# A four-layer block on one core: modulation sums moved to TensorE, a norm read from PSUM, and two mixers in another order

## Chip, core and metric

The kernel runs on one core of one Trainium2 chip. The metric is the device time of one execution in microseconds (us). Engine names in the profile: PE is TensorE's matmuls, PEld its weight loads, DVE is VectorE, ACT is ScalarE, POOL is GpSimd, SP is SyncE, which issues most DMAs. SBUF is the memory that the engines work in, PSUM the one that TensorE writes to. "us" and "ns" are as printed.

## What is computed

A sequence of 512 tokens of width 1024 goes through four layers: one of differential attention beside a long convolution, one of multi-scale pooling, each with an MLP, and then two hybrid layers, each with a recurrent unit (RG-LRU) beside latent attention, and a gated feed-forward part. Everything is fp32. Of the reference, cut to what the change touches:

```python
def _modulate(h, shift, scale):
    return h * (1 + scale) + shift
...
    s_lat = jax.nn.silu(c)
    s_ctx = jax.nn.silu(c_ctx)
...
        mod_l = [m[:, None, :] for m in jnp.split(s_lat @ ada_w[i] + ada_b[i], N_MOD, axis=-1)]
        a_lat = _modulate(_rmsnorm(h_lat, norm1_g[i]), mod_l[0], mod_l[1])
...
            mod_c = jnp.split(s_ctx @ ada_w[i] + ada_b[i], N_MOD, axis=-1)
            a_ctx = _modulate(_rmsnorm(h_ctx, norm1_g[i]), mod_c[0], mod_c[1])
...
            p_lat = a_lat @ mix_w_in[e] + mix_b_in[e]
            q_l = _axial_rope(_split_q(p_lat), row, col)
            k_l, v_l = _split_kv(p_lat[..., KV_START:HY_START])
...
            k_c, v_c = _split_kv(kv_ctx)
            k_all = jnp.concatenate([k_c, k_l], axis=1)
            v_all = jnp.concatenate([v_c, v_l], axis=1)
            att_l = _diff_post(_diff_attn_blocked(q_l, k_all, v_all, lam), subln_g[e], lam_init)
...
def rg_lru(x, positions, w_a, b_a, w_x, b_x, a_param):
...
    mult = jnp.where(reset, 1.0, jnp.sqrt(-jnp.expm1(2.0 * log_a)))
    b_in = xf * i * mult
...
    _, h = lax.associative_scan(combine, (a, b_in), axis=1)
...
    y = jax.nn.sigmoid(gate_a) * y_a + jax.nn.sigmoid(gate_b) * y_b
```

## The kernel before

Activations lie transposed: a tile is 128 features by 512 tokens, eight tiles to the sequence. Each fp32 value is split into a high part and a rest, and a product is three matmuls, high by high, rest by high and high by rest (`mm3`, L458 to L460). Weights come from HBM in raw blocks of 512 KB through a ring of six buffers (`RAW_BUFS`), issued by SyncE in one order (`_dma_to`); ScalarE casts the high part (`_emit_h`, L255) and VectorE or GpSimd subtract the rest (`_emit_l`, L273). A buffer is issued anew when its block's part is done (`_done_part`). Big PSUM tiles are called `ps`; there are two small ones, `pss`. The order of the instructions on an engine is that in which the program is written; the table `PR` says at many places which of VectorE (V), GpSimd (G) and ScalarE (A) takes an operation, and how many steps of a side task run at a point.

**Modulation.** The sums `s_lat @ ada_w` come in halves of 512 columns. For each half four raw blocks of two slices come through the same ring; each slice of 128 by 512 is scaled by one column of `s_lat` and added to an accumulator (`_ada_step`, `scaled`, `add_scaled`: L371 on GpSimd, L373 on ScalarE, addition L383 on GpSimd). At the end VectorE transposes and reduces (`ada_sums`, L416 and L418), and TensorE puts the sums into columns (`flush`). Halves 4 to 9 of layer 0 run this way among the projections and the attention loop, one part whenever a weight is taken.

**The start.** `start` reads the tokens (x) and the context (ctx), takes statistics over eight tiles k, and sums the first shift, which needs the scaling of 32 slices, on GpSimd, VectorE and ScalarE by turns (L369, L371, L373, L378, L383). Then the reciprocal root (`rsqrt`) is broadcast by TensorE into PSUM and copied to SBUF (rb, rc), the shift's columns are summed (L1104, then `sh`, L1107), and the norm runs in passes: VectorE multiplies the eight tiles (L1120), ScalarE makes the high part (L1129), GpSimd and VectorE a second copy (L1130), and the rest is subtracted (L1124). After that come six outputs `out` and the eight context tiles (L1141 to L1144).

**Layer 0.** The query columns are computed in one gemm, then each of four keys with the sequence's tiles and, at once, with the context's. `v_shift` sums a shift for the values over eight tiles. Then an attention loop of 16 steps s follows: scores (L1500, L1505), the weights normalised and combined (`combine1`, L1527 and L1528), at every other step the transposes of the weights into two `pss` and one `ps` (L1541), their split (L1548, L1553), the product with the values, and one fill gemm of the long convolution's columns (`gemm1`).

**The hybrid mixers.** `conv2` and `conv` project and convolve, `lru_mm` makes the two gates of one block of the recurrent unit, `lru_exp` its decay (three operations of VectorE, L1977 to L1979), `lru_sqrt` the multiplier (ScalarE, L1986, with a table load), `lru_scan` the recurrence (VectorE, L1991). Two norms of the latents need a reciprocal root each (`rsqrt`, L548 to L556, ending in the tile ny; broadcast L563). Then eight heads run: a gate's gemm (`gate`, ScalarE's sigmoid L2101), the weights' transposes (`trans`), the next head's scores (softmax L2051 to L2056), a second gate, the product `pv`, and in even heads a query gemm split by L526 and L527. The four roots 0 to 3 stand ahead of the head loop, the scans 0 to 3 in head 0, roots 4 to 7 in head 1 and scans 4 to 7 in head 2.

## Time and profile before

| | us |
|---|---|
| median of 3 runs | 2636.95 (2635.93 to 2643.82) |
| profiled execution | 2637.4 |
| its span in the trace | 2635.6 |
| TensorE busy | 2467.1 (94%) |
| VectorE busy | 1826.1 (69%) |
| ScalarE busy | 1166.9 (44%) |
| GpSimd busy | 1413.7 (54%) |
| mean granted clock of TensorE, of full speed | 0.959 |

The start runs to about 130 us, projections of layer 0 to about 190, the attention loop to about 390, the rest of its mixer to about 450. The hybrid mixers lie at about 1230 to 1520 and 1940 to 2220 us. In a row of the timeline "x4" means four instructions of one line in a row, whose time is given from the first's start to the last's end; a bracket gives the time that the engine was idle before and what released it. A matmul's end is modelled, so that its pace is read from the starts.

### The profile page before, as it was taken

What the parts mean: (1) busy time and instruction counts of PE and PEld (TensorE: products, weight loads), DVE (VectorE), ACT (ScalarE), POOL (GpSimd) and SP (SyncE); (2) the same over time, 40 slices, a digit from 0 to 9 for tenths busy, and PEclk for the clock granted to TensorE, in tenths of its full rate; (3) what the DMA queues carried; (4) which work ended last, traced back from release to release, by engine and by line L of the source; (5) the groups of instructions that cost most, each with busy time, mean ns of one, the idle gap of its engine ahead of it and who ended that gap; (6) DMA issues with size and microseconds to landing.
All of it is one profiled execution on the core that took longest, in us unless ns stands there. A gap on an engine that the chain in (4) does not pass through costs nothing.

```text
span 2635.6 us, 32004 instructions
## 1 busy us (share of the span) xinstructions
PE 2467.1 (94%) x11496; PEld 2060.0 (78%) x11496; DVE 1826.1 (69%) x2649; ACT 1166.9 (44%) x2153; POOL 1413.7 (54%) x1120
## 2 busy tenths in 40 slices
PE   8787877999999999999879999999998899999998
PEld 6666666888888788888768888888887788888887
DVE  6899987786657797767788676455577876743334
ACT  3445653554434533335466544222346654523231
POOL 6687746277652489954564437878137735230001
PEclk8788988999999999999989999999989999999999
DMA  7233422376672366662212336666422123353321
GB/s 245 83 123 95 127 81 80 94 203 197 201 221 68 97 176 206 208 176 77 95 50 67 104 88 184 184 188 196 118 85 73 55 78 112 94 154 96 96 86 51
DMA packets 433367, 330.29 MB, mean 125 GB/s; under 512 B 11799, under 2 KB 365207, under 8 KB 433208
## 3 DMA queue, kind: packets, MB, share of 16 engines
q1 hardware_dynamic: 429976, 322.22, 41.2%
q0 software_dynamic: 3232, 6.03, 0.7%
q8 instruction: 90, 1.47, 0.2%
q14 instruction: 69, 0.57, 0.1%
HBM read 319.82 MB, written 8.39 MB: 125 GB/s over the span
## 4 chain that ended last, share of the span: by engine, by line
PE 71%; DVE 20%; ACT 3%; issue 3%; DMA 1%; POOL 1%; SPq 0%; DVEq 0%; ACTq 0%; POOLq 0%
PE ps L458 20%; PE ps L459 20%; PE ps L460 20%; PE ps L619 5%; PE ps L477 4%; DVE slot L273 1%; DVE slot L1991 1%; DVE slot L527 1%; DVE slot L1943 1%; PE ps L1385 1%; DVE slot L1553 1%; DVE slot L2056 1%; PE pss L574 1%; DVE slot L1979 1%; DVE mx L1501 1%
## 5 line engine op out<-in xcount | busy, mean ns | idle before, releaser
L458 PE MATMUL ps<-slot 128*128 128x512 f32 (+1 forms) x3024 | 1164.2, 385 | 55.3 <-DVE slot L527 16.8
L460 PE MATMUL ps<-slot 128*128 128x512 f32 (+1 forms) x3024 | 1156.1, 382 | 21.4 <-DVE slot L527 9.2
L459 PE MATMUL ps<-slot 128*128 128x512 f32 (+1 forms) x3024 | 1155.2, 382 | 3.9 <-POOL slot L273 1.7
L458 PEld LDWEIGHTS ps<-slot 128*128 128x128 f32 x3024 | 580.6, 192 | 168.7 <-DVE slot L527 19.6
L460 PEld LDWEIGHTS ps<-slot 128*128 128x128 f32 x3024 | 579.2, 192 | 131.5 <-DVE slot L527 9.5
L459 PEld LDWEIGHTS ps<-slot 128*128 128x128 f32 x3024 | 580.1, 192 | 109.0 <-POOL slot L273 2.6
L383 POOL TENSOR_TENSOR slot<-slot 128x512 f32<-128x512 f32 x336 | 490.0, 1458 | 128.2 <-ACT slot L373 102.5
L255 ACT CAST slot<-raw 128x512 fp32r<-128x512 f32 (+1 forms) x764 | 426.2, 614 | 271.3 <-DMA raw<-in_mlp_w_dram 147.9
L273 DVE TENSOR_TENSOR slot<-raw,slot 128x512 fp32r<-128x512 f32 x588 | 497.7, 891 | 24.4 <-ACT slot L255 23.1
L542 POOL TENSOR_TENSOR slot<-slot 128x512 f32<-128x512 f32 (+1 forms) x64 | 92.1, 1443 | 510.0 <-ACT slot L536 509.6
L273 POOL TENSOR_TENSOR slot<-raw,slot 128x512 fp32r<-128x512 f32 (+1 forms) x176 | 252.3, 1458 | 175.1 <-ACT slot L255 135.0
L371 POOL TENSOR_SCALAR slot<-raw,cols 128x512 f32<-128x512 f32 x192 | 199.5, 1042 | 117.1 <-DMA raw<-in_w_ada_dram 57.3
L536 ACT ACTIVATE slot<-slot 128x512 f32<-128x512 f32 (+1 forms) x98 | 55.4, 577 | 223.8 <-DVE slot L1716 69.4
L619 PE MATMUL ps<-slot 128*128 128x512 f32 x576 | 145.9, 413 | 6.0 <-DVE slot L1821 6.0
L371 POOL TENSOR_SCALAR slot<-raw,s_lat 128x512 f32<-128x512 f32 x96 | 113.8, 1189 | 62.2 <-DMA raw<-in_ada_w_dram 23.2
L2204 DVE TENSOR_TENSOR slot<-slot,ps 128x512 f32<-128x512 f32 x40 | 27.5, 688 | 172.1 <-PE ps L460 172.1
L619 PEld LDWEIGHTS ps<-slot 128*128 128x128 f32 x576 | 114.0, 200 | 31.5 <-DVE slot L1821 7.4
L526 ACT CAST slot<-slot 128x512 fp32r<-128x512 f32 x80 | 47.2, 622 | 182.5 <-DVE slot L2204 154.0
L477 PE MATMUL ps<-slot 128*128 128x512 f32 x480 | 111.1, 390 | 4.1 <-ACT slot L526 2.8
L477 PEld LDWEIGHTS ps<-slot 128*128 128x128 f32 x480 | 89.7, 188 | 23.8 <-ACT slot L526 3.2
L1716 DVE SCALAR_TENSOR_TENSOR slot<-ps,mod,slot 128x512 f32<-128x512 f32 x64 | 47.7, 746 | 82.0 <-PE ps L460 82.0
L527 DVE TENSOR_TENSOR slot<-slot 128x512 fp32r<-128x512 f32 x75 | 77.8, 1057 | 37.2 <-ACT slot L526 37.2
(321 smaller groups left out, 2768.0 us busy)
## 6 DMA issues: line engine op xcount, KB each, us to landing
raw<-in_mlp_w_dram SPq DMA_DIRECT2D x128, 512.0 KB, 5.3
raw<-in_w_ada_dram SPq DMA_DIRECT2D x96, 512.0 KB, 4.4
raw<-in_ada_w_dram SPq DMA_DIRECT2D x88, 512.0 KB, 4.6
raw<-in_w_ffn_in_dram SPq DMA_DIRECT2D x88, 512.0 KB, 4.4
raw<-in_w_in_dram SPq DMA_DIRECT2D x56, 512.0 KB, 3.8
raw<-in_w_ffn_out_dram SPq DMA_DIRECT2D x32, 512.0 KB, 5.1
raw<-in_mix_w_dram SPq DMA_DIRECT2D x20, 512.0 KB, 3.8
raw<-in_w_out_dram SPq DMA_DIRECT2D x16, 512.0 KB, 4.0
```

Source lines behind the costliest of these rows:

```text
L255: self.S.copy(r(v), src[:, k:k + kk, :])
L273: eng.tensor_tensor(r(lv), src, v, op=ALU.subtract)
L371: self.G.tensor_scalar(out, x, sc, 0.0, op0=ALU.mult, op1=ALU.add)
L383: self.G.tensor_tensor(out, out, v, op=ALU.add)
L458: self.PE.matmul(out, lhsT=wh, rhs=xh, start=start, stop=False)
L459: self.PE.matmul(out, lhsT=wl, rhs=xh, start=False, stop=False)
L460: self.PE.matmul(out, lhsT=wh, rhs=xl, start=False, stop=stop)
L477: self.PE.matmul(ps[:], lhsT=w[k][i], rhs=xs[k][j], start=(k == 0 and n == 0), stop=(k == kc - 1 and n == 2))
L527: (eng or self.V).tensor_tensor(r(l)[:, 0:n], src, h[:, 0:n], op=ALU.subtract)
L536: self.S.activation(sq[:, 0:n], x, AF.Square, scale=scale)
L542: (eng or self.G).tensor_tensor(st["acc"][:, 0:n], st["acc"][:, 0:n], sq[:, 0:n], op=ALU.add)
L619: PE.matmul(ps[:], lhsT=w[i][:, m * 128:(m + 1) * 128], rhs=r(x[j])[:], start=(k == 0 and n == 0), stop=(k == 7 and n == 2))
```

## The change

**Layer 0's modulation.** For halves 4 to 9 `_ada_rows` multiplies a raw slice on TensorE: the column of `s_lat` is broadcast to 32 stationary columns and the slice of 512 columns streams past; four slices go to the four 32-row parts of one `pss`. These are jobs: `gemm1` and the keys let one matmul of them in after every second k (`work(1)`) and what is left at the end. ScalarE copies the finished tile, and later `_ada_cols` adds the four parts up with 128 by 1 matmuls against `sel4`, two new columns of the constants. A raw block stays open until its job is done, which holds back the issue of the block that would take its buffer.

**The start.** The first shift is scaled by ScalarE and added by GpSimd; the value shift too. The norm goes tile by tile: VectorE multiplies by the broadcast in PSUM, ScalarE makes the high part, ScalarE or VectorE the copy in turns, VectorE the rest. The query columns and three keys run together over k, then the fourth key; the context's keys come last.

**The mixers.** One `rsqrt` over eight columns takes the place of two, its broadcast stands one gemm later; the roots, the exponentials and the scans are spread over the heads.

```diff
-    fs='GGVA',
-    vs='VA',
-    fstep=(1, 2, 1, 0, 0, 1, 0, 3),
+    fs='AAAA',
+    vs='AA',
+    fstep=(0, 1, 1, 0, 1, 2, 2, 1),
...
     def _done_part(self, p):
-        self._dma_to(p["idx"] + RAW_BUFS)
+
+        self.dma_want = max(self.dma_want, p["idx"] + RAW_BUFS)
+        self._dma_to(min([self.dma_want] + [i + RAW_BUFS - 1 for i in self.open]))
...
-        if kind == "ada":
+        if kind == "ada" and extra[0] == 0 and 4 <= extra[1] < 10:
+            self.open.append(p["idx"])
+            self.jobs.append(self._ada_rows(p, *extra[1:]))
+        elif kind == "ada":
...
+    def _ada_rows(self, p, half, i):
...
+        if i % 2 == 0:
+            self.bank = self.ps_s.tile([128, 512], F32, tag="pss", name="pss")
+        ps = self.bank
+        for k in range(2):
+            q = 2 * (i % 2) + k
+            self.PE.matmul(ps[32 * q:32 * q + 32, :], lhsT=self.s_lat[:, 2 * i + k:2 * i + k + 1].to_broadcast([128, 32]), rhs=p["raw"][:, k, :], start=True, stop=True)
+            yield
+        self.open.remove(p["idx"])
+        self._done_part(p)
+        if i % 2:
+            t = self.get()
+            self.S.copy(t[:], ps[:])
+            self.defer(lambda: self._ada_cols(t, half, i))
...
+    def _ada_cols(self, t, half, i):
+        ps = self.ps_s.tile([128, 512], F32, tag="pss", name="pss")
+        for j in range(4):
+            self.PE.matmul(ps[:, j:j + 1], lhsT=t[:, j * 128:(j + 1) * 128], rhs=self.sel4[:, 0:1], start=True, stop=True)
+        self.put(t)
+        m = self.mod[0][:, half * 4:half * 4 + 4]
+        self.V.tensor_tensor(m, ps[:, 0:4], self.col("ada_b", half * 4, 4) if i == 1 else m, op=ALU.add)
...
         for k, x in enumerate(xs):
             self.mm3(ps[:], w[k], x, k == 0, k == len(xs) - 1)
+            if k % 2:
+                self.work(1)
+        self.work()
...
-        bp, rb = self.bcast(y, 4, self.ps_s, "pss"), self.get()
-        S.copy(rb[:], bp[:])
-        bp, rc = self.bcast(y[:, 4:6], 2, self.ps_s, "pss"), self.get()
-        S.copy(rc[:, 0:TC], bp[:, 0:TC])
+        self.prefetch(3)
...
+        def norm(x, f, n, c_, hi, lo, k):
...
+            V.tensor_tensor(t[:, 0:n], x, f, op=ALU.mult)
+            S.activation(r(hi), t[:, 0:n], AF.Identity, scale=sc, bias=b)
+            if k % 2:
+                V.tensor_scalar(z[:, 0:n], t[:, 0:n], sc, b, op0=ALU.mult, op1=ALU.add)
+            else:
+                S.activation(z[:, 0:n], t[:, 0:n], AF.Identity, scale=sc, bias=b)
+            V.tensor_tensor(r(lo), z[:, 0:n], hi, op=ALU.subtract)
...
+        pss = keys(ws[0:3])
+        self.put(ws[0].tiles)
+        zq(0, pss[0])
+        for j in range(2):
+            ropes.append(self.rope(pss[1 + j], bin_(4 + j), rope))
+        ropes.append(self.rope(keys(ws[3:4])[0], bin_(6), rope))
...
-        yq = self.rsqrt(self.stat_ms(stq, 256, 1e-6), 4)
-        yk = self.rsqrt(self.stat_ms(stk, 128, 1e-6), 4)
         conv(2)
+        y = latent_rstd()
         lru_mm(0)
-        bq, bk = self.bcast(yq, 4), self.bcast(yk, 4)
         conv(3)
+        bq, bk = self.bcast(y, 4), self.bcast(y[:, 4:8], 4)
...
-        lru_sqrt(range(4))
...
             PT = trans(P)
+            if hd in (0, 3):
+                lru_sqrt(range(4) if hd == 0 else range(4, 8))
             P = scores(hd + 1) if hd < 7 else None
-            if hd < 2:
-                lru_exp(2 * hd + 4)
-                lru_exp(2 * hd + 5)
+            if hd in (1, 2):
+                lru_exp(2 * hd + 2)
+                lru_exp(2 * hd + 3)
             gb = gate()
-            if hd == 0:
-                lru_scan(range(4))
-            elif hd == 1:
-                lru_sqrt(range(4, 8))
-            elif hd == 2:
-                lru_scan(range(4, 8))
+            lru_scan(((0,), (1, 2), (3,), (4,), (5,), (6,), (7,), ())[hd])
```

How the rows of the engines move, at three places. Line numbers of the changed kernel are higher by 3 to 81 than those of before.

TensorE, the end of a fill gemm in the attention loop and the start of the product with the values behind it, before:

```order
L458 MATMUL ps<-slot 128x512
L459 MATMUL ps<-slot 128x512
L460 MATMUL ps<-slot 128x512
L458 MATMUL ps<-slot 128x256
L459 MATMUL ps<-slot 128x256
```

and now (L502 to L504 are `mm3`, L403 is `_ada_rows`):

```order
L403 MATMUL pss<-raw,s_lat 32x512
L502 MATMUL ps<-slot 128x512
L503 MATMUL ps<-slot 128x512
L504 MATMUL ps<-slot 128x512
L502 MATMUL ps<-slot 128x512
L503 MATMUL ps<-slot 128x512
L504 MATMUL ps<-slot 128x512
L403 MATMUL pss<-raw,s_lat 32x512 x5
L502 MATMUL ps<-slot 128x256
```

A raw slice now stands after every six matmuls of the gemm, and what is left of the jobs, five here, behind its last. Of the 48 such matmuls 12 come in the projections and 36 in the fill gemms of steps 1, 3, 5, 7, 9 and 13; 24 of the 48 stand in runs of four or five.

VectorE, the first head of a hybrid mixer between the softmax (its scaling L2056, now L2124) and the split of the query gemm (L527, now L574), before:

```order
L2056 TENSOR_SCALAR slot<-slot,sm_12200 128x512
L1977 TENSOR_TENSOR slot<-slot 128x512
L1978 SCALAR_TENSOR_TENSOR slot<-slot 128x512
L1979 SCALAR_TENSOR_TENSOR slot<-slot 128x512
L1977 TENSOR_TENSOR slot<-slot 128x512
L1978 SCALAR_TENSOR_TENSOR slot<-slot 128x512
L1979 SCALAR_TENSOR_TENSOR slot<-slot 128x512
L1991 SCALAR_TENSOR_TENSOR slot<-slot 128x512 x4
L527 TENSOR_TENSOR slot<-ps,slot 128x512 x2
```

and now:

```order
L2124 TENSOR_SCALAR slot<-slot,sm_12214 128x256
L2124 TENSOR_SCALAR slot<-slot,sm_12214 128x384
L2124 TENSOR_SCALAR slot<-slot,sm_12214 128x512
L2059 SCALAR_TENSOR_TENSOR slot<-slot 128x512
L574 TENSOR_TENSOR slot<-ps,slot 128x512 x2
```

Two exponentials' chains and three of four scans have left the place ahead of the split; the chains stand in heads 1 and 2 now.

ScalarE, around the roots (L1986, now L2054), the first gate (L2101, now L2182) and the casts of the weights' transposes (L2080, now L2148), before:

```order
L1961 ACTIVATE slot<-ps,cols 128x512 x4
L1986 ACT_TABLE_LOAD
L1986 ACTIVATE slot<-slot 128x512 x4
L255 CAST slot<-raw 128x512
L2101 ACT_TABLE_LOAD
L2101 ACTIVATE slot<-ps 128x512
L1961 ACTIVATE slot<-ps,cols 128x512 x2
L2080 CAST slot<-pss 128x512
```

and now:

```order
L2029 ACTIVATE slot<-ps,cols 128x512 x4
L258 CAST slot<-raw 128x512
L2182 ACTIVATE slot<-ps 128x512
L2029 ACTIVATE slot<-ps,cols 128x512 x2
L2148 CAST slot<-pss 128x512
L2148 CAST slot<-ps 128x384
L2148 CAST slot<-pss 128x256
L2148 CAST slot<-ps 128x128
L2054 ACT_TABLE_LOAD
L2054 ACTIVATE slot<-slot 128x512 x4
L2121 ACT_TABLE_LOAD
```

The four roots have moved behind the gate and the transposes, and the gate's table load ahead of the sigmoid is gone here.

## Rows read from the trace of the kernel before

**Rows 1.** The page's head: span, and each engine's busy time, share and instructions.
```profile
span 2635.6 us, 32004 instructions
PE 2467.1 (94%) x11496; PEld 2060.0 (78%) x11496; DVE 1826.1 (69%) x2649; ACT 1166.9 (44%) x2153; POOL 1413.7 (54%) x1120
```

**Rows 2.** Windows: stretch, us; busy (count) of PE, PEld, DVE, ACT, POOL; clock; DMA.
```profile
130.00:190.00 60.00, 49.32 (x224) 40.87 (x223) 59.14 (x74) 26.14 (x46) 52.03 (x36) 0.81 0.40 132
190.00:390.00 200.00, 160.74 (x773) 132.69 (x771) 180.81 (x297) 121.33 (x276) 126.92 (x101) 0.89 0.31 95
1230.00:1520.00 290.00, 260.20 (x1268) 218.65 (x1269) 220.33 (x366) 174.46 (x329) 153.50 (x126) 0.95 0.26 78
1940.00:2220.00 280.00, 255.93 (x1244) 215.23 (x1243) 213.26 (x332) 174.95 (x330) 153.12 (x127) 0.96 0.27 81
```

**Rows 3.** Waits of TensorE, 85 to 450 us: total, times, longest.
```profile
PE pss L1541 <- DVE slot L1528: 15.6, 4, 10.4
```

**Rows 4.** Timeline of VectorE: start, us, engine, line, operation.
```profile
127.28 2.49 DVE L527 TENSOR_TENSOR slot<-slot 128x512 fp32r<-128x512 f32 x4
157.43 5.83 DVE L527 TENSOR_TENSOR slot<-slot 128x512 fp32r<-128x512 f32 x4
```

**Rows 5.** Groups of GpSimd, 130 to 440 us: busy, mean ns, idle before.
```profile
L383 POOL TENSOR_TENSOR slot<-slot 128x512 f32<-128x512 f32 x49 | 72.0, 1471 | 35.3 <-ACT slot L373 31.8
L371 POOL TENSOR_SCALAR slot<-raw,s_lat 128x512 f32<-128x512 f32 x32 | 33.7, 1055 | 0.0
```

**Rows 6.** Timeline of the start: ScalarE, VectorE, TensorE.
```profile
72.28 5.01 ACT L373 ACTIVATE slot<-raw,s 128x512 f32<-128x512 f32 x8
...
87.31 7.33 DVE L378 SCALAR_TENSOR_TENSOR slot<-raw,s,slot 128x512 f32<-128x512 f32 x6
98.31 0.24 DVE L1107 TENSOR_TENSOR sh<-pss,cols 128x8 f32<-128x8 f32 x2 [3.66 <-PE pss L1104]
98.46 4.71 DVE L1120 TENSOR_TENSOR slot<-slot 128x512 f32<-128x512 f32 x7
...
113.42 1.22 DVE L1124 TENSOR_TENSOR slot<-slot 128x512 fp32r<-128x512 f32 x1 [0.68 <-POOL slot L1130]
...
126.94 0.43 DVE L1144 TENSOR_TENSOR slot<-slot 128x256 fp32r<-128x256 f32 x1
...
120.27 0.39 PE L460 MATMUL ps<-slot 128*128 128x512 f32 x1
```

**Rows 7.** Timeline of TensorE: fp32 matmuls in the input stage, start and value shift.
```profile
18.07 1.07 PE L920 MATMUL pss<-slot,hw 33*64 33x512 f32 x2
19.07 0.50 PE L458 MATMUL ps<-slot 128*128 128x512 f32 x1
...
88.65 1.95 PE L1104 MATMUL pss<-ones,slot 128*128 128x1 f32 x16 [0.46 <-ACT slot L1096]
...
190.45 1.88 PE L1169 MATMUL pss<-slot,ones 128*128 128x512 f32 x4
```

**Rows 8.** Waits of TensorE, first mixer; the last row: second mixer.
```profile
PE ps L458 <- DVE slot L527: 8.4, 4, 6.7
PE ps L458 <- ACT slot L2101: 7.4, 1, 7.4
PE ps L563 <- DVE ny L556: 6.4, 2, 5.4
...
PE ps L458 <- DVE slot L527: 8.4, 4, 6.6
```

**Rows 9.** Timeline of the first hybrid mixer's first head: ScalarE, VectorE, TensorE.
```profile
1340.87 0.63 ACT L1986 ACTIVATE slot<-slot 128x512 f32<-128x512 f32 x1 [2.37 <-DVE slot L1979]
...
1360.48 8.71 DVE L1991 TENSOR_TENSOR_SCAN slot<-slot 128x512 f32<-128x512 f32 x4
...
1369.83 0.58 PE L458 MATMUL ps<-slot 128*128 128x256 f32 x1 [6.67 <-DVE slot L527]
...
1374.79 0.39 PE L458 MATMUL ps<-slot 128*128 128x512 f32 x1
```

More of the change, by code (lines that the diff above doesn't have):

```diff
@@ L384, in add_scaled, with work @@
             self.put(t)
+    def _ada_rows(self, p, half, i):
[19 more added lines that the diff above has]
+        self.V.tensor_tensor(m, ps[:, 0:4], self.col("ada_b", half * 4, 4) if i == 1 else m, op=ALU.add)
+        if i == 3:
+            self.ready.add((0, half))
+    def work(self, n=None):
+        while self.jobs and n != 0:
+            if next(self.jobs[0], self) is self:
+                self.jobs.pop(0)
+            elif n:
+                n -= 1
     def _ada_step(self, p, layer, half, i):
@@ L520, in gemm1 @@
             self.mm3(ps[:], w[k], x, k == 0, k == len(xs) - 1)
+            if k % 2:
+                self.work(1)
+        self.work()
         self.put(w.tiles)
@@ L1131, in start @@
             A.append(hl)
             self.put(xs[k])
[L1133 to L1135 removed]
+            if k in (2, 4):
+                out(1 + k // 2)
+        bp = self.bcast(y[:, 4:6], 2, self.ps_s, "pss")
+        for i in range(4, 6):
             out(i)
[L1137 to L1138 removed]
+        self.prefetch(4)
         for k in range(8):
[L1140 to L1144 removed]
+            p = self.get()
+            norm(cx[k], bp[:, 0:TC], TC, 1, p[:, 0:TC], p[:, TC:2 * TC], k)
@@ L1145, in start @@
             AC.append(p)
-            self.put(t)
-        self.put(rc)
+        self.put(cxt)
         self.sh = sh
-        self.put(cxt)
-        next(self.filt)
         self.vw = vw
@@ L1220, in zq, with keys @@
             self.defer(lambda: Q.__setitem__(j, self.stack_put(a, True)), PR["zqd"])
-        zq(0, gemm1("q"))
+        look, self.look = self.look, 0
+        ws, ropes = [self.consume(n) for n in ("q", "k", "k", "k")], []
+        def keys(ws):
+            pss = [self.ps() for _ in ws]
+            for k in range(8):
+                for w, ps in zip(ws, pss):
+                    self.mm3(ps[:], w[k], axs[k], k == 0, k == 7)
+                if k % 2:
+                    self.work(1)
+            self.work()
+            return pss
+        pss = keys(ws[0:3])
[4 more added lines that the diff above has]
+        ropes.append(self.rope(keys(ws[3:4])[0], bin_(6), rope))
         self.l_eng = V
@@ L1232, in layer0 @@
             self.put(w.tiles)
-            a = self.rope(ps, bin_(4 + j), rope)
+            if j == 1:
+                self.prefetch(1)
+                for _ in range(8 - 2 * len(PR["tapk"])):
+                    next(self.filt)
+                next(self.filt)
+            a = ropes[j]
             t = self.get()
@@ L2096, in pv, with latent_rstd @@
             return po
+        def latent_rstd():
+            ps, ms = self.ps_s.tile([128, 512], F32, tag="pss", name="pss"), self.small(8, "ms8")
+            for i, st in enumerate((stq, stk)):
+                for t in range(4):
+                    PE.matmul(ps[:, 4 * i + t:4 * i + t + 1], lhsT=st["acc"][:, t * 128:(t + 1) * 128], rhs=self.ones[:, 0:1],
+                              start=True, stop=True)
+                self.put(st["acc"])
+            for i, width in enumerate((256, 128)):
+                cs = slice(4 * i, 4 * i + 4)
+                V.tensor_scalar(ms[:, cs], ps[:, cs], 1.0 / width, 1e-6, op0=ALU.mult, op1=ALU.add)
+            return self.rsqrt(ms, 8)
         def gate():
```

55 lines of the change are left out of this document (24 added, 31 removed).

## The prediction, made before the changed kernel ran

> **What bounds the kernel now.** I read the head of the page first, then the stage windows, then TensorE's waits, then single operations at the places of the edits. TensorE is busy 2467.1 of 2635.6 us [rows 1], so only some 168 us can be won without taking work from it. The windows show where these lie [rows 2]: of 130 to 190 us TensorE works 49.32, of 190 to 390 us 160.74, and there VectorE is the full engine (59.14 of 60, 180.81 of 200) with GpSimd busy for most of the time beside it (52.03 and 126.92). The two hybrid mixers leave it idle for 29.8 and 24.1 us. The longest kind of wait in layer 0 is that of the attention transposes for the weights that VectorE combines, 15.6 us in four pieces [rows 3]: VectorE sets the pace there.
>
> VectorE is slow because of GpSimd: the same four subtractions took 2.49 us at 127.28, when GpSimd was at rest, and 5.83 us at 157.43 beside it [rows 4]. That is 0.84 us more for one.
>
> **Modulation sums on TensorE.** The six halves are 24 raw blocks, 48 slices of 512 columns. Off GpSimd go 32 scalings of 1.055 us, 33.7 us, and of the 49 additions in the stretch some 35 (14 stay or come for the value shift) of 1.471 us, 51 us [rows 5]. From VectorE go twelve transposes and reductions (0.62 us each at the best, by the uncontended four of [rows 4]: 7.5 us) and eight steps of the value shift at 7.33 / 6 = 1.22 us [rows 6], 10 us. And each of 67 removed GpSimd operations may have held VectorE up by 0.84 us, at most 56 us; operations that read PSUM do not show the effect and part of GpSimd's time falls beside those, so I take half, 28 us, and keep 0 and 56 as ends. VectorE gets 17.5 + 28 = 46 us lighter, less twelve small additions, out of 240 us in 130 to 390 us.
>
> TensorE pays. No fp32 matmul with 32 output columns is in the trace; the nearest is L920 with 64 columns between two full matmuls. It starts at 18.07 and the next one at 19.07: 1.0 us. Two 128-column ones (L1169) took 1.88 us, 0.94 each [rows 7]. I take 1.0 because L920 has the narrow output and the neighbours of this case, 48 x 1.0 = 48 us. The 48 one-column matmuls that turn rows into columns are like L1104: 16 records, which are 8 matmuls of two passes each, in 1.95 us, so 0.24 us each and 12 us. Together 60 us, from 57 to 70.
>
> The Trainium skill speaks against this edit: its page TensorEngine Tiling (Array Packing), section Key Properties, says that a change of the tiling mode drains TensorE, and here single 32-column matmuls stand between 128-column ones. The trace shows what such a switch costs at L920: the matmul behind it took 0.50 us [rows 7] where its like takes 0.39 at full clock [rows 9], which would make 5 us more for 48 of them, within my upper end.
>
> Is there room? In 130 to 390 us TensorE is idle 260 - 210.06 = 50 us, and loses 0.19 of 49.32 and 0.11 of 160.74, 27 us, to a granted clock of 0.81 and 0.89 [rows 2], which comes back if it is kept busy. So 77 us of room for 60 us, if the waits on VectorE shrink by its 46 us. Then the loop is almost full on TensorE (143 + 48 = 191 of 200 at full clock), and no shorter than now. Two added waits work against it: a sum holds one of only two small PSUM buffers until ScalarE's copy, and the transposes of the weights, queued behind on TensorE, want both; and a raw block stays in the ring of six until its matmuls, so SyncE's next weight load waits. The DMA share of 0.31 to 0.40 in this stretch [rows 2] covers the second one. I put the loop at 0, from 12 us shorter to 15 us longer.
>
> **The start.** The first shift is now scaled by ScalarE alone (20 scalings behind the last input, of 5.01 / 8 = 0.63 us) and added by GpSimd alone, 18 additions of 1.471 us = 26.5 us. ScalarE begins at 72.28, so the sums come at about 100, where VectorE ended at 87.31 + 7.33 = 94.6 and the shift stood at 98.31 [rows 6]. With what ScalarE and GpSimd no longer do ahead of it this is a loss of some 2 us; the ends are 3 us won and 8 lost.
>
> The norm then reads the broadcast from PSUM and no GpSimd operation is left in it. Before, the eight tiles took from 98.46 to 113.42 + 1.22 = 114.6, and the context ones to 127.4 [rows 6]: 28.9 us. Now VectorE has 16 operations of 0.67 us (4.71 / 7 in the same rows), four of 0.7, then 16 of 0.43 and four of 0.4: 13.5 + 8.5 = 22 us, a gain of 7. The q columns and three keys run together over the tiles, so that by the end of the norm 96 full matmuls are done where 48 were done at 120.27; then VectorE's wait for context tiles no longer stops TensorE. That is worth at most 48 x 0.23 = 11 us, of which I take 6, since VectorE is the full engine behind it and 12 raw matmuls now stand there. Sum: 7 + 6 - 2 = 11 us won, from 0 to 20.
>
> **The hybrid mixers.** Their waits for other engines are listed in [rows 8]. The longest, 7.4 us in each mixer, is a gate's output that ScalarE could not take because four square roots stood ahead of it, and these waited for VectorE: the last began at 1340.87 after 2.37 us of it [rows 9]. Now the roots stand behind the weights' transposes of the first head, when their inputs are long done, and ScalarE has lost the two pairs of exponentials of that head: I take 6 of 7.4. The second, 6.7 us, is for a subtraction behind four scans (8.71 us from 1360.48) and two exponential chains of VectorE ahead of them. Now one scan is there and the chains are gone to the next two heads, where two scans at most stand in a row: 4.5 of 6.7. The third is the first mixer's reciprocal root: two chains in turn become one of the same length over eight columns, 4 of 6.4. After such a gap TensorE was at half clock, from 1369.83 to 1374.79 [rows 9], which loses half of 5 us; 3 us per mixer for its two gaps. That gives 4 + 6 + 4.5 + 3 = 17.5 and 6 + 4.5 + 3 = 13.5; less 1 us each for new small waits, 29 us. Ends: 16 us, if the moved chains and roots stop the next heads, and 36.
>
> **At nothing:** the wider constant and its small DMA (beside loads of weights), four squares' additions on VectorE in the input stage, and two table loads fewer per mixer on ScalarE, which isn't full. If uncovered, the squares cost 4 x 0.7 = 3 us.
>
> **Sum.** 11 + 0 + 29 = 40 us off the profiled 2637.4 us (2635.6 us and 1.8 around it): 2597 us. The median of the runs is 2636.95, half a microsecond off, which I leave.
>
> **Rivals.** (1) The hybrid gaps only move: VectorE has the same work in 290 us and has 220.33 of it now [rows 2]; chains and scans of the later heads come to stand before subtractions that TensorE wants. Then 8 of 29 remain: 2618 us. Against it: the waits are of bursts, not of a full engine. Chance 0.12. (2) GpSimd's leaving doesn't speed VectorE, as its ScalarE-fed additions for the value shift stay beside it: VectorE then gets only 17 us lighter, the loop is held by both, 12 us longer, 2609 us. Against it: the two rows of [rows 4]. Chance 0.09. (3) Runs of four and five raw matmuls at the ends of gemms overlap, each in its own 32 columns: 24 of the 48 would take the time of 6, 18 us less on TensorE, of which the loop gives back 12: 2585 us. Nothing in the trace has such neighbours. Chance 0.10. The same page and section of the Trainium skill says that different tiles can run matmuls in parallel; no row here shows it. (4) The slower side: TensorE becomes the bound of layer 0. The raw matmuls stand inside the gemms whose results the next scores wait for, in order, and the two small PSUM buffers force the transposes to wait for sums. If none of the 60 us falls into the idle 50, all are added: 2597 + 60 = 2657 us. It decides from 40 us on the path; 48 make it slower by 0.3%. For it: DMA, copy and buffer tie the engines closely. Against it: VectorE gets lighter in the same stretch. Chance 0.07. The forecast has 0.62.
>
> **Range and chances.** The bounds of the three terms give 2637 - 20 - 12 - 36 = 2569 and 2637 + 15 - 16 = 2636; not all fall together, and I take 2572 to 2624, which holds rivals 1, 2 and 3 as well and leaves out the slower one and corners of the forecast, some 0.2. A measurement of this kernel can tell 0.3% from no change, 7.9 us. The forecast puts 0.60 of its 0.62 on faster, rival 1 0.11, 2 0.07, 3 0.10: 0.88 faster, 0.06 the same, 0.06 slower.
>
> **What would show it.** Right: TensorE over 0.93 busy at a clock near 0.95 from 190 to 390 us with the loop's end within 15 us of before, a 32-column matmul of about 1.0 us start to start, GpSimd's busy time in 130 to 390 us down by some 80, the four subtractions nearer 2.5 us, the context tiles' norm ended by about 121, and no wait over 3 us in the hybrid mixers. Wrong: the transposes waiting for sums' buffers by tens of microseconds; shift sums past 108; new waits of 5 us in heads 1 to 3.

## The result, and the profile after

The changed kernel takes 2661.7 us (median of 4 runs, 2657.3 to 2664.6) against 2637.4 us of before in the same comparison: ratio 1.0087, 95% interval 1.0072 to 1.0101. It is 24 us slower. The forecast was 2597 us and faster, and the time lies above the whole range.

The head of the page after (busy us, share of the span, instructions), to be read against [rows 1]:

```profile
span 2662.6 us, 32281 instructions
PE 2502.4 (94%) x11680; PEld 2065.7 (78%) x11680; DVE 1790.1 (67%) x2630; ACT 1183.0 (44%) x2183; POOL 1286.0 (48%) x1018
```

The stage windows after (stretch, us; busy us and count of PE, PEld, DVE, ACT, POOL; clock; DMA share; GB/s), to be read against [rows 2]:

```profile
130.00:190.00 60.00, 38.78 (x177) 27.45 (x175) 49.47 (x67) 34.60 (x62) 27.07 (x17) 0.80 0.17 55
190.00:390.00 200.00, 174.66 (x826) 126.78 (x826) 129.42 (x273) 106.51 (x242) 49.53 (x41) 0.92 0.30 92
1230.00:1520.00 290.00, 268.34 (x1300) 225.53 (x1299) 237.05 (x362) 170.71 (x317) 162.57 (x128) 0.96 0.25 73
1940.00:2220.00 280.00, 263.46 (x1275) 221.43 (x1274) 223.76 (x346) 168.50 (x319) 150.28 (x121) 0.96 0.26 77
```

The relief came as forecast: VectorE, busy before for 180.81 of the 200 us from 190 to 390, is busy for 129.42 of them, and GpSimd for 49.53. But TensorE lost 10.5 us of work in 130 to 190 us, and has 14 us more in the loop, with the added matmuls. What it waits for in layer 0 (85 to 450 us: total, times, longest):

```profile
PE ps L502 <- ACT slot L573: 19.3, 1, 19.3
PE pss L403 <- issue: 14.9, 5, 7.8
PE pss L1150 <- POOL slot L392: 12.8, 1, 12.8
PE ps L504 <- DVE slot L574: 7.9, 1, 7.9
```

The 15.6 us of the transposes [rows 3] are gone. The first two lines are new: a gemm that waits for a cast on ScalarE (L573), and the raw matmuls themselves (L403).

When each stage starts, against before, for the same matmul in both traces: the first scores begin at 206.58 instead of 177.58 (+29.0), layer 0 ends 41 us later, the first hybrid mixer gives back about 5 and the second about 9, and the end is 27.0 us later (spans 2662.6 and 2635.6). Nearly all of the miss is in layer 0. I call "shift of layer 0" how much later the same gemm matmul, counted from the first, starts behind layer 0, some 455 us into before; it comes from one profiled execution of each kernel.

### The profile page after: what moved, and what is told of

The parts are those of the page before. It is cut to its first block, busy times and chain, and to the rows that moved or that the text cites. A ratio compares the mean times of both kernels' runs of the same rounds, so it can differ in the third digit from the quotient of the medians.

```text
span 2662.6 us, 32281 instructions
## 1 busy us (share of the span) xinstructions
PE 2502.4 (94%) x11680; PEld 2065.7 (78%) x11680; DVE 1790.1 (67%) x2630; ACT 1183.0 (44%) x2183; POOL 1286.0 (48%) x1018
## 4 chain that ended last, share of the span: by engine, by line
PE 75%; DVE 14%; ACT 5%; issue 3%; DMA 1%; POOL 1%; SPq 0%; DVEq 0%; ACTq 0%; POOLq 0%
PE ps L502 21%; PE ps L503 21%; PE ps L504 21%; PE ps L666 4%; PE ps L521 3%; PE pss L403 1%; DVE slot L2011 1%; DVE slot L279 1%; DVE slot L2047 1%; PE pss L621 1%; PE ps L1453 1%; DVE slot L574 1%; ACT slot L258 1%; ACT slot L716 1%; PE ps L2115 1%
## 5 line engine op out<-in xcount | busy, mean ns | idle before, releaser
L502 PE MATMUL ps<-slot 128*128 128x512 f32 (+1 forms) x3024 | 1167.7, 386 | 48.3 <-ACT slot L573 19.3
L504 PE MATMUL ps<-slot 128*128 128x512 f32 (+1 forms) x3024 | 1153.9, 382 | 8.6 <-DVE slot L574 7.9
L502 PEld LDWEIGHTS ps<-slot 128*128 128x128 f32 x3024 | 580.0, 192 | 186.9 <-issue 24.1
L504 PEld LDWEIGHTS ps<-slot 128*128 128x128 f32 x3024 | 578.9, 191 | 116.8 <-DVE slot L574 8.1
L392 POOL TENSOR_TENSOR slot<-slot 128x512 f32<-128x512 f32 x308 | 452.5, 1474 | 163.3 <-ACT slot L382 142.8
L589 POOL TENSOR_TENSOR slot<-slot 128x512 f32<-128x512 f32 (+1 forms) x60 | 82.8, 1384 | 507.4 <-ACT slot L583 507.0
L573 ACT CAST slot<-slot 128x512 fp32r<-128x512 f32 x80 | 47.3, 619 | 191.6 <-DVE slot L2280 153.9
L380 POOL TENSOR_SCALAR slot<-raw,s_lat 128x512 f32<-128x512 f32 x64 | 77.8, 1220 | 61.5 <-DMA raw<-in_ada_w_dram 23.2
L574 DVE TENSOR_TENSOR slot<-slot 128x512 fp32r<-128x512 f32 x75 | 79.4, 1079 | 36.6 <-ACT slot L573 36.6
```

The lines of the kernel that those rows point to most:

```text
L380: self.G.tensor_scalar(out, x, sc, 0.0, op0=ALU.mult, op1=ALU.add)
L392: self.G.tensor_tensor(out, out, v, op=ALU.add)
L502: self.PE.matmul(out, lhsT=wh, rhs=xh, start=start, stop=False)
L504: self.PE.matmul(out, lhsT=wh, rhs=xl, start=False, stop=stop)
L574: (eng or self.V).tensor_tensor(r(l)[:, 0:n], src, h[:, 0:n], op=ALU.subtract)
L589: (eng or self.G).tensor_tensor(st["acc"][:, 0:n], st["acc"][:, 0:n], sq[:, 0:n], op=ALU.add)
```

## Experiments

**The three edits alone.** Each of these is the kernel before with one edit. In the first, `_ada_rows`, `_ada_cols` and `work` of the change, with the keys of the old projection order:

```diff
             self.mm3(ps[:], w[k], x, k == 0, k == len(xs) - 1)
+            if k % 2:
+                self.work(1)
+        self.work()
```

> The kernel before with the modulation sums on TensorE alone: start, order of the projections, engine table and mixers as before, the raw matmuls let into gemms and keys after every second k. Theory A (TensorE's order and the two small PSUM buffers cost more than VectorE's relief brings): 12 to 18 us longer, 2650 to 2655 us, with waits of the raw matmuls of about 15 us in the attention loop. Theory B (the loss in layer 0 is that of the start, which moves the whole loop; the sums by themselves give what GpSimd and VectorE lose): 10 us shorter or more, 2627 us.

Measured: 2658.2 us, ratio 1.0068 [1.0051, 1.0086], +17 us; layer 0 shifts by +22. VectorE falls to 125.35 us busy in 190 to 390 us and TensorE rises to 175.43. The relief is there, and the kernel is slower all the same, with TensorE the busy engine. That is my fourth rival, in part.

The second has the start: the first shift on ScalarE and GpSimd, the norm tile by tile, the projections' order, and with it the filter's steps behind the keys. Three entries of the table `PR` go with it: the query weights' subtractions (`l_q`) move from GpSimd to VectorE and the side task's steps are spread otherwise (`side`), neither of which I had priced, and the squares of the statistics (`sx`, `sc`) all go to VectorE, which I had put at nothing. None of them was run alone.

```diff
-    fs='GGVA',
+    fs='AAAA',
...
+            V.tensor_tensor(t[:, 0:n], x, f, op=ALU.mult)
+            S.activation(r(hi), t[:, 0:n], AF.Identity, scale=sc, bias=b)
...
+            V.tensor_tensor(r(lo), z[:, 0:n], hi, op=ALU.subtract)
```

> The kernel before with the changed start alone: first shift on ScalarE and GpSimd, norm tile by tile from PSUM, keys together, context keys last, filter steps behind them, engine table; sums on GpSimd and ScalarE and mixers as before. In the trace of the changed kernel the norm ends 13.5 us later and one wait of 19.3 us for the filter's split stands behind it. Theory A (the parts add): the first scores come 25 us later or more, and the whole is 20 to 30 us longer, 2660 us. Theory B (VectorE and GpSimd catch up in the attention loop, which was bound by them): 5 to 10 us longer, 2645 us. The forecast had 11 us shorter.

Measured: 2661.9 us, 1.0074 [1.0055, 1.0092], +21 us; layer 0 +26. My 11 us won were 26 lost. TensorE's waits of this run, 85 to 450 us:

```profile
PE ps L494 <- ACT slot L562: 22.1, 1, 22.1
PE pss L1596 <- DVE slot L1583: 13.0, 6, 8.0
PE pss L1137 <- POOL slot L384: 12.8, 1, 12.8
```

L494 and L562 are the lines of `mm3` and of the cast here: the long wait belongs to the start's edit, with no raw matmul on TensorE. The third has the mixers' edit:

```diff
-            if hd < 2:
-                lru_exp(2 * hd + 4)
-                lru_exp(2 * hd + 5)
+            if hd in (1, 2):
+                lru_exp(2 * hd + 2)
+                lru_exp(2 * hd + 3)
...
+            lru_scan(((0,), (1, 2), (3,), (4,), (5,), (6,), (7,), ())[hd])
```

> The kernel before with the change of the two hybrid mixers alone (one reciprocal root, roots, exponentials and scans spread). My forecast was 29 us shorter. The trace of the changed kernel has the matmuls of the first mixer come 5 us nearer to those of before over that mixer and those of the second 8.6 us nearer. Theory A (the three parts add): 13 to 14 us shorter, 2624 us. Theory B (the mixers are disturbed by what layer 0 leaves behind, the ring of raw blocks above all): 25 us or more shorter, 2612 us.

Measured: 2617.2 us, 0.9912 [0.9895, 0.9929], 24 us faster, near the forecast of 29. In its trace the mixers give 7 and 12 us.

**What a raw matmul costs.** Two stretches of TensorE in the kernel after (start, us, engine, line, operation and tile):

```profile
177.90 0.28 PE L504 MATMUL ps<-slot 128*128 128x256 f32 x1
178.11 1.06 PE L403 MATMUL pss<-raw,s_lat 128*32 128x512 f32 x8
179.10 0.50 PE L502 MATMUL ps<-slot 128*128 128x512 f32 x1
...
180.36 0.40 PE L504 MATMUL ps<-slot 128*128 128x512 f32 x1
180.69 1.04 PE L403 MATMUL pss<-raw,s_lat 128*32 128x512 f32 x2
181.67 0.50 PE L502 MATMUL ps<-slot 128*128 128x512 f32 x1
182.00 0.40 PE L503 MATMUL ps<-slot 128*128 128x512 f32 x1
```

Two records are one fp32 matmul. Four in a row take 1.06 us, one alone takes 1.04: the four run side by side, each in its own 32 columns. The one alone also costs around it: from 180.36 to 182.00 are 1.64 us for it and two 128-column matmuls, which without it start 0.23 us apart, so about 1.2 us are its own. The Trainium skill's page TensorEngine Tiling (Array Packing), section Key Properties, says that different tiles can execute matmuls in parallel, and that a change of the tiling mode drains TensorE. This trace agrees: four cost one, and around a single one some 0.2 us are lost beside its own 0.98 from start to start; that this loss is the drain, no run shows. So the next run leaves the arithmetic as it is and lets the raw matmuls stand only behind a whole gemm:

```diff
             self.mm3(ps[:], w[k], x, k == 0, k == len(xs) - 1)
-            if k % 2:
-                self.work(1)
         self.work()
```

> As the one with the sums on TensorE alone, but no raw matmul stands inside a gemm: all that are ready run behind it, four or eight in a row. In the trace of the changed kernel four in a row took 1.08 us from start to the next matmul's start (178.02 to 179.10), as much as one by itself, so that TensorE would pay 12 times 1.1 us instead of 24 times 1.2 us and 5 runs, some 25 us less. Theory A (the price on TensorE and in its order decides): 15 to 25 us shorter than with single ones. Theory B (the small PSUM buffers decide, which are asked for as often): within 5 us of it.

Measured: 2625.0 us, 0.9941 [0.9920, 0.9961], 16 us faster than before and 33 us faster than the singles; layer 0 -11. Its raw matmuls now stand in runs such as:

```profile
161.60 0.39 PE L504 MATMUL ps<-slot 128*128 128x512 f32 x1
161.92 1.92 PE L403 MATMUL pss<-raw,s_lat 128*32 128x512 f32 x16
163.77 0.38 PE L502 MATMUL ps<-slot 128*128 128x256 f32 x1
```

Eight in 1.85 us. Is it the overlap, or that the sums' small PSUM buffers are asked for at better times? The same kernel with 128 equal columns for each raw matmul keeps the place and takes the overlap away (the four parts of a bank then overwrite each other):

```diff
-            self.PE.matmul(ps[32 * q:32 * q + 32, :], lhsT=self.s_lat[:, 2 * i + k:2 * i + k + 1].to_broadcast([128, 32]), rhs=p["raw"][:, k, :], start=True, stop=True)
+            self.PE.matmul(ps[:], lhsT=self.s_lat[:, 2 * i + k:2 * i + k + 1].to_broadcast([128, 128]), rhs=p["raw"][:, k, :], start=True, stop=True)
```

> As the kernel with the sums in runs behind the gemms, but each raw matmul has 128 stationary columns instead of 32, over the whole small buffer, so that none can run beside another; each overwrites the one before, so the halves' sums are not those of the reference. Theory A (the gain of the runs is TensorE's time: four at a time against one after the other): 48 times 0.86 us = 41 us on TensorE in place of some 13, so 20 to 28 us longer than with 32 columns, 2648 us, as much as with single ones. Theory B (the gain is that of the small buffers, which are held for a shorter time): within 6 us of the narrow one, 2628 us.

Measured: 2646.1 us, 1.0028 [1.0016, 1.0040], +7.5 us. By the ratios 23 of the 33 us are lost again, with the raw matmuls where they were; by the shifts of layer 0 (+6 against -11) it is 17. Its rows:

```profile
163.04 0.39 PE L504 MATMUL ps<-slot 128*128 128x512 f32 x1
163.26 7.03 PE L403 MATMUL pss<-raw,s_lat 128*128 128x512 f32 x16
169.73 0.68 PE L502 MATMUL ps<-slot 128*128 128x256 f32 x1
```

Eight take 6.47 us instead of 1.85. The three kernels make a ledger. Column two adds up every stretch of L403 from its first start to the next matmul's start; three is the L403 wait of the list of waits; the 48 column matmuls (L415) are 11 us in each, 0.23 each by the 1.84 us that eight took in the kernel after:

| kernel | 48 raw matmuls, us | their waits | all added | shift of layer 0 | won on the path |
|---|---|---|---|---|---|
| sums_only | 37.1 | 14.2 | 62 | +22 | 40 |
| sums_wide_grouped | 39.7 | 2.8 | 53 | +6 | 47 |
| sums_grouped | 11.4 | 3.5 | 26 | -11 | 37 |

The last column is what GpSimd's and VectorE's relief was worth: 37 and 40 us with 32 columns, and 47 in the wide kernel. There TensorE was granted 0.94 and 0.95 of its clock in 130 to 190 and 190 to 390 us, in sums_grouped 0.91 and 0.92; by my estimate from these that is 8 of the 10 us between the two. So the relief differs less than the price, 62, 53 or 26 us, and the price sets the sign. Of the 33 us between singles and runs, 17 to 23 are lost with the overlap; the rest goes with the waits, 14.2 us against 3.5 and 2.8, and with the switches, which the wide matmuls, of as many columns as their neighbours, don't have either. The longest of the waits, in the kernel after, is this one:

```profile
246.90 1.03 PE L403 MATMUL pss<-raw,s_lat 128*32 128x512 f32 x1 [7.83 <-issue]
```

and VectorE, at the same time:

```profile
245.73 0.47 DVE L1596 SCALAR_TENSOR_TENSOR slot<-slot,rc 128x256 f32<-128x256 f32 x1
246.12 1.27 DVE L1621 TENSOR_TENSOR slot<-pss,slot 128x512 fp32r<-128x512 f32 x2
```

The first raw matmul of a sum opens a small buffer. Both were held by transposes whose subtraction (L1621) stood behind the softmax on VectorE; when the first of the two was done, at about 246.8, TensorE went on. The profile names no releaser ("issue"); that it is the buffer is read from this coincidence and from the tile's name, pss. I had foreseen the transposes waiting for the sums. It was the other way round, inside a gemm, with everything of TensorE queued behind.

**The start.** VectorE in the norm after (the bracket is the idle time before, and what ended it):

```profile
104.04 0.24 DVE L1153 TENSOR_TENSOR sh<-pss,cols 128x8 f32<-128x8 f32 x2 [0.24 <-PE pss L1150]
105.06 0.69 DVE L1165 TENSOR_TENSOR slot<-slot,pss 128x512 f32<-128x512 f32 x1 [0.79 <-PE pss L610]
107.40 0.69 DVE L1171 TENSOR_TENSOR slot<-slot 128x512 fp32r<-128x512 f32 x1 [1.65 <-ACT slot L1170]
108.01 0.68 DVE L1165 TENSOR_TENSOR slot<-slot,pss 128x512 f32<-128x512 f32 x1
108.72 0.55 DVE L1168 TENSOR_SCALAR slot<-slot,gg,sh 128x512 f32<-128x512 f32 x1
109.68 0.69 DVE L1171 TENSOR_TENSOR slot<-slot 128x512 fp32r<-128x512 f32 x1 [0.41 <-ACT slot L1166]
...
125.33 0.69 DVE L1171 TENSOR_TENSOR slot<-slot 128x512 fp32r<-128x512 f32 x1 [0.36 <-ACT slot L1166]
```

A tile's subtraction (L1171) follows its multiplication (L1165) on the same engine and needs ScalarE's two results of it, so VectorE stands still for 1.65 us on every second tile and about 0.4 on the others. From 104.04 to the end of the last subtraction are 22.0 us, 21.0 of them from the first multiplication on, and the context tiles take to 140.85. The waits ahead of L1171 add up to 8.1 us in the eight tiles and 5.7 in the context's. Two theories of the 29 us: this chain, or the filter's cast behind it. In the first kernel each subtraction is issued behind the next tile's multiplication:

```diff
-            V.tensor_tensor(r(lo), z[:, 0:n], hi, op=ALU.subtract)
-            self.put(t, z)
+            self.put(t)
+            if late:
+                late.pop()()
+            def rest():
+                V.tensor_tensor(r(lo), z[:, 0:n], hi, op=ALU.subtract)
+                self.put(z)
+            late.append(rest)
```

> The changed kernel with one thing altered in the start: VectorE's subtraction of a tile is issued behind the multiplication of the next tile. In the trace of the changed kernel VectorE waits for ScalarE's copy in every tile, and the eight tiles take 22.0 us, the context's 13.7. Theory A (that order is the whole of it): 14 to 16 us and 9 to 10 us, the norm's end 10 us earlier, the wait for the filter's split the same or longer, so 3 to 10 us shorter in all. Theory B (ScalarE with its 12 operations of 0.8 us and the outputs is the bound): under 3 us earlier.

Measured: 2646.8 us in one run, 15 us less than the median of the kernel after and 11 less than its fastest run; layer 0 +31 instead of +41, and the first scores at 196.2 instead of 206.58. So 10 us of it are in layer 0; the rest lies behind it, where the two kernels are one. The eight tiles run from 107.29 to 120.07, 12.8 us instead of 21.0, close to my 13.5:

```profile
110.24 0.68 DVE L1165 TENSOR_TENSOR slot<-slot,pss 128x512 f32<-128x512 f32 x1
110.83 0.69 DVE L1176 TENSOR_TENSOR slot<-slot 128x512 fp32r<-128x512 f32 x1
111.44 0.68 DVE L1165 TENSOR_TENSOR slot<-slot,pss 128x512 f32<-128x512 f32 x1
```

The second kernel moves the value shift's filter steps back between the norms:

```diff
+        for _ in range(8 - 2 * len(PR["tapk"])):
+            next(self.filt)
         bp = self.bcast(y[:, 4:6], 2, self.ps_s, "pss")
```

> The changed kernel with the filter's steps put back where they were, between the norm of the tiles and that of the context, instead of after the second context key. In the trace of the changed kernel TensorE waits 19.3 us there for ScalarE's cast of the filter, which waits for VectorE, which has the ropes and the stacking of the keys ahead of it, slowed by GpSimd's additions for the value shift. Theory A (the place makes that wait): the wait falls under 5 us, the first scores come 15 us earlier. Theory B (VectorE has the same work to do before the scores wherever it stands): the wait goes to the ropes, and the first scores come within 5 us of where they are.

Measured: 2651.4 us in one run, 10 us less than the median of after and 6 less than its fastest run; layer 0 +34, the first scores at 199.2, 7 us earlier. The wait for the cast is gone and another stands there:

```profile
PE pss L502 <- DVE slot L1165: 18.3, 1, 18.3
```

The filter's matmul now waits for the small buffer in which the broadcast lies until the norm's last multiplication. Before, a copy in SBUF had freed that buffer at once. The wait of after itself comes from VectorE's order. TensorE's row:

```profile
166.34 0.80 PE L502 MATMUL ps<-slot 128*128 128x512 f32 x1 [19.30 <-ACT slot L573]
```

ScalarE's row, the cast that it waits for:

```profile
165.15 1.66 ACT L573 CAST slot<-slot 128x512 fp32r<-128x512 f32 x3 [4.21 <-DVE slot L928]
```

And what VectorE does ahead of L928:

```profile
153.47 1.75 DVE L1509 TENSOR_TENSOR slot<-slot 64x512 fp32r<-64x512 f32 x1
155.23 1.66 DVE L1511 TENSOR_TENSOR slot<-slot 64x512 fp32r<-64x512 f32 x1
```

The cast needs L928, and L928 stands behind ropes and their stacking (the same two lines again until 160.2), which run beside six GpSimd additions (149.76 to 159.68) at 1.7 us instead of the 0.67 to 0.69 that the same lines took at 247.92.

A third kernel gives the first shift its old engines:

```diff
-    fs='AAAA',
+    fs='GGVA',
...
-    fstep=(0, 1, 1, 0, 1, 2, 2, 1),
+    fstep=(1, 2, 1, 0, 0, 1, 0, 3),
```

> The changed kernel with the first shift by engines and steps as before (GpSimd, VectorE and ScalarE by turns), all else as changed. In the trace of the changed kernel GpSimd adds 18 times in a row, 76.59 to 102.04, and TensorE waits 12.8 us for it; the shift stands at 104.04 where it stood at 98.31. Theory A (that chain makes the shift late): the shift stands at 98 to 100 and the norm ends 5 us earlier. Theory B (VectorE's steps come back behind the reciprocal root, which GpSimd slows): within 2 us.

Measured: 2667.1 us in one run; layer 0 +44. The shift stood at 107.2 there, later than the 104.04 of after. But this run moved more than the chain: its reciprocal root began at 91.51, where that of after began at 80.72 and that of before at 80.91. So it can't tell what the chain did in after. The rows of after and before can, for the column sums that the shift is made of, on TensorE:

```profile
100.43 3.58 PE L1150 MATMUL pss<-ones,slot 128*128 128x1 f32 x16 [12.82 <-POOL slot L392]
94.70 3.57 PE L1104 MATMUL pss<-ones,slot 128*128 128x1 f32 x16 [4.11 <-DVE slot L378]
```

They start 5.7 us later, as the shift does, and wait for the GpSimd chain, whose last addition ends at 102.04. The chain alone need not be the whole of it: VectorE was until 103.80 at six subtractions of weights, which the changed start takes ahead of the shift (7.96 us beside the chain, 3.70 in shift_back, where GpSimd was at rest); before had two there, on GpSimd. Why the root came 11 us later in shift_back was not traced.

**Put together.** The sums in runs with the mixers' edit, and the start of before, that is both of these against before:

```diff
+        self.work()
...
+        y = latent_rstd()
```

> The kernel before with the sums on TensorE in runs behind the gemms and the changed mixers, without the changed start. Apart they were 16 us and 24 us shorter than before. Theory A (they are in different stages and add): 36 to 44 us shorter, 2600 us. Theory B (GpSimd's and VectorE's place ahead of the mixers shifts with layer 0, so that the mixers win less, as in the changed kernel, where they won 14): 28 to 32 us shorter.

Measured: 2612.4 us, 0.9900 [0.9882, 0.9918], 26 us faster than before. That is less than either theory. Beside sums_grouped the mixers add 10 us, each median against its own before, or 19 by the spans of the two traces, where the execution of sums_grouped was the slowest of its four; the 24 lie outside both. The same with the norm read from PSUM and its subtraction one tile behind, in the old projection order:

```diff
-            self.eng("ax").tensor_tensor(xs[k][:], xs[k][:], rb[:], op=ALU.mult)
...
+            norm(xs[k][:], bp[:], T, 0, hl[0][:], hl[1][:], k)
...
+        late.pop()()
```

> The kernel with the sums in runs and the changed mixers, and the norm read tile by tile from PSUM, but with VectorE's subtraction one tile behind, the order of the projections and the engine table as before, and the filter's steps behind the first key. With the subtraction one tile behind the eight tiles took 12.8 us (107.29 to 120.07) where before had 16.2, and the context's 10.8. Theory A (the norm is on the path to the first scores): the first scores come 5 us earlier than before or more, and the whole is 4 to 8 us shorter than without it, 2606 us. Theory B (VectorE is full up to the first scores, and the filter's steps that moved behind the norm take what it gave): within 3 us of it.

Measured: 2608.7 us, 0.9883 [0.9862, 0.9904], 30 us faster than before, the fastest of all; but 4 us from the one above, within its interval, with layer 0 at -13 against -12. The norm from PSUM, free of its waits, is worth next to nothing here. And sums_grouped_mixers with the reciprocal roots in two chains, as before:

```diff
+        yq = self.rsqrt(self.stat_ms(stq, 256, 1e-6), 4)
+        yk = self.rsqrt(self.stat_ms(stk, 128, 1e-6), 4)
...
-        y = latent_rstd()
```

> The kernel with the sums in runs and the changed mixers, but with two reciprocal roots of four columns where they stood before. In the trace of the changed kernel TensorE waits 8.7 and 3.3 us for the single root, where it waited 6.4 and 1.5 us for two. Theory A (ten small operations of VectorE in a row that each wait for a GpSimd operation are as bad as twenty, and later): the same or up to 4 us shorter than with one. Theory B (one chain less is what the forecast said): 4 us longer.

Measured: 2618.1 us, 0.9922 [0.9906, 0.9938]. One chain for two is worth about 6 us by the medians beside sums_grouped_mixers, 5 by the spans of the traces and 4 behind layer 0; the two intervals overlap a little. Last, the kernel after with nothing changed but raw matmuls only in runs, in the keys' loop and here:

```diff
             self.mm3(ps[:], w[k], x, k == 0, k == len(xs) - 1)
-            if k % 2:
-                self.work(1)
         self.work()
```

> The changed kernel with one thing altered: no raw matmul inside a gemm, all in runs behind it. Against the kernel before the same alteration was worth 33 us. Theory A (it is worth as much here): 25 to 35 us shorter than the changed kernel, 2632 us. Theory B (here the start's waits hide a part, as the raw matmuls of the projections fall into them): 15 to 25 us shorter.

Measured: 2635.7 us, 0.9992 [0.9981, 1.0004]: 26 us less than after, and no difference from before that can be told. Layer 0 is at +17. The rest of the start's loss is still there, with its wait for the cast at 20.8 us.

## Why the prediction was wrong

**GpSimd and VectorE: right.** I had VectorE 46 us lighter in 130 to 390 us. It fell by 61 us there (59.14 + 180.81 to 49.47 + 129.42), part of it because work moved out of these windows; in sums_grouped, whose layer 0 ends earlier, it fell by 30. On the path the relief was worth 37 to 40 us.

**The price on TensorE: right in sum by accident.** Single matmuls cost about 1.2 us as against 1.0, each of a run of four a quarter, and the runs of five 1.83 us. In the kernel after the 48 come to 33 us, not 48; the columns were 11 us (I had 12); and 15 us are waits for small buffers, which I had named and not priced. 59 us in all against my 60.

**The room: wrong.** The step that failed is "77 us of room for 60 us". I added TensorE's idle time, which the VectorE waits had caused, and a clock gain, and so set 60 against 60. The room that the relief gave was 37 to 40 us, so in sums_only 22 of the 62 us stayed on the path. The clock did come back from 190 to 390 us (0.89 to 0.92), but only by 0.03 of 200 us, 6 us; from 130 to 190 us, where TensorE stood for 19.3 us, it was 0.80 after 0.81. In the kernel after the loop and its tail cost 12 us beyond the start's 29; I had 0, with 15 as the upper end. My fourth rival had the mechanism and too small a chance. The third rival is shown: the columns run side by side, and four cost one. I had left its gain to the runs at the gemms' ends and didn't ask what it meant for the other half: every single one gives it away.

**The start: wrong, the largest step.** Forecast 11 us won, measured 26 us lost alone by the shift of layer 0, 21 by the medians, and 29 at the first scores in the kernel after. Three terms failed. (a) I summed VectorE's 40 operations to 22 us for both norms; they took 36.8 us (104.04 to 140.85), and 13.8 of these are waits for ScalarE inside the tiles, which VectorE, working in order, could not fill. With the subtraction one tile behind, the eight tiles took 12.8 us. (b) The shift stood 5.7 us later (98.31 to 104.04) where I had 2. My own figures had put the sums at about 100 instead of 94.6; I took that down to 2 us without a row, and priced neither the root, which took 11.6 us beside the chain where it took 4.2 before, nor the six subtractions of weights ahead of the shift. (c) I priced no wait for the filter steps that moved behind the keys; TensorE then stood for 19.3 us. (a) and (c) were each shown by a run, 10 and 7 us at the first scores, single runs both, and they overlap: with the norm's waits gone, the wait for the cast was 11.1 us. For (b) the rows show the chain as what the sums waited for; no run shows the share of each edit.

**The mixers: right in kind, sized too large.** By the medians 24 us of my 29 when alone; 13 to 14 by the trace in the kernel after. The wait for the gate's output [rows 8, 9] is gone, as forecast. TensorE's waits of 1230 to 1540 us after begin with

```profile
PE ps L610 <- DVE ny L603: 8.7, 1, 8.7
PE ps L503 <- POOL slot L279: 2.9, 2, 2.2
PE ps L2134 <- DVE slot L2239: 2.6, 1, 2.6
PE ps L502 <- DVE slot L2149: 2.4, 1, 2.4
```

The reciprocal root's wait has grown from 6.4 [rows 8] to 8.7 us, where I took 4 us won. VectorE at that place:

```profile
1311.67 2.31 DVE L2011 SCALAR_TENSOR_TENSOR slot<-ps,cols,slot 128x511 f32<-128x511 f32 x3
1313.89 0.22 DVE L2176 TENSOR_SCALAR ms<-pss 128x4 f32<-128x4 f32 x2
...
1317.39 0.17 DVE L601 TENSOR_TENSOR na<-ny 128x8 f32<-128x8 f32 x1
1317.59 1.12 DVE L602 SCALAR_TENSOR_TENSOR nb<-na,ms 128x8 f32<-128x8 f32 x1
1318.75 1.18 DVE L603 SCALAR_TENSOR_TENSOR ny<-nb,ny 128x8 f32<-128x8 f32 x1
```

Yet two chains were 4 to 6 us slower in a run, so the longer wait replaces a longer sum of work: a wait's length is no measure of what its removal gives. That the mixers gave only about half beside the other edits is not borne out. mixers_only shows the same waits as after, 8.7, 2.9, 2.6 and 2.4 us. From behind layer 0 to the matmul that starts 2600 us into before the traces have 2145 us in before, and 2147 to 2149 in the four kernels with other sums or another start and the old mixers. With the changed mixers they have 2124 in mixers_only, and in company 2124 to 2126 in norm_pipelined, after_grouped and filter_back, but 2131 to 2132 in after, shift_back, best_norm and sums_grouped_mixers. So the edit gave 21 us alone, and 14 or 20 to 21 in company, with one code. The granted clock parts the two groups: what it was short of full, times the time, makes 27 to 29 us over this stretch in the slower four and 22 to 24 in the other four, which by this estimate is most of the 7 us between them. In before it makes 38, in part while TensorE was idle, so some of what the mixers gave is clock as well. Why the clock was granted otherwise with one code stays open, and these are single executions. My first rival, gaps that only move, isn't needed for it.

In the profiled times layer 0 is 52 us worse than forecast (+41 for -11) and the mixers 15 to 16 worse. That makes 67 to 68 us, and the profiled run is 2664.6 against 2597. Some 7 us of the mixers' part are that difference of clock.

## What to carry to other kernels

Small-column matmuls that can run side by side belong in runs of as many as there are column groups; one at a time between wide ones they cost here the full price and the switch, and that alone turned a gain of 16 us into a loss of 17. When a stall is paid for with work on the engine that stalled, count the relief on the path once, not the idle time and the stall and the clock. On an engine that works in order, don't sum durations of a step that passes through another engine and back: either issue the return one tile later, or add the other engine's time for every tile; and for each step that is moved, look what stands ahead of it in its new place.

## What the runs showed of the hardware that I had not expected

- Four fp32 matmuls of 32 columns by 512 into the four quarters of a PSUM bank took 1.06 us, one took 1.04; eight took 1.85, and eight of 128 columns 6.47 at the place that was compared, at the full clock.
- Single VectorE operations on 128 x 8 elements took 0.17 us, or 1.12 to 1.19 us when GpSimd was at tiles of 128 x 512 (a subtraction at 1317.43, then five in 6.14 us, 1318.65 to 1324.79): a small operation lost about 1 us, as much as one on 128 x 512 did at 1.7 instead of 0.68. In the start the nine steps of the reciprocal root, on 128 x 6, took 1.19 to 1.22 us each beside the new chain of 18 GpSimd additions, which lies across them. The Trainium skill, SBUF — State Buffer, section Who interferes with whom, says that a VectorE instruction with two SBUF inputs contends with a GpSimd instruction that reads SBUF; these rows agree, and give the price for a tiny one.
